# Two decoder layers on one core: the mixers rebuilt with transposed projections, heads on halves and quarters of the matmul array, gates spread by DMA, a new order and a new beginning

## Chip, core and metric

The kernel runs on one core of a Trainium2 chip. The metric is the device time of one execution in microseconds; lower is better. The core has a matmul engine (TensorE, PE in the profile, its weight loads PEld), a vector engine (VectorE, DVE), an engine for functions and copies (ScalarE, ACT), a general one (GpSimd, POOL) and one that issues DMAs (SyncE, SP). Matmuls read SBUF and write PSUM, which has eight banks of 128 x 512 fp32 here.

## The reference

x has 256 positions of width 1024. Each of two layers has three parts; ahead of each stands an RMS norm, behind each another, whose output is added to x.

```python
for l in range(DEPTH):                                   # 2
    h = rms_norm(x, pre_mix_g[l])
    x = x + rms_norm(parallel_mixer(h, ...), post_mix_g[l])
    h = rms_norm(x, pre_cross_g[l])
    x = x + rms_norm(memory_cross_attention(h, mem_n, ...), post_cross_g[l])
    h = rms_norm(x, pre_ffn_g[l])
    x = x + rms_norm(swiglu(h, w_gate[l], w_up[l], w_down[l]), post_ffn_g[l])

# parallel_mixer
lx, ly, fq, fk, fv, ff, rq, rk, rv, rg = split(h @ w_in)   # widths 256, 256, 512, 512, 512, 8, 256, 256, 256, 256
lru_out = rg_lru(causal_conv(lx), ...) * gelu(ly)          # gates of 4 blocks of 64, then a scan over positions
fox_out = forgetting_attention(fq, fk, fv, ff, ...)        # 8 heads of 64
ret_out = retention(rq, rk, rv, rg, positions)             # 4 heads of 64, rotary, decay, norm per head
return concat(lru_out, fox_out, ret_out) @ w_out

# forgetting_attention
c = cumsum(log_sigmoid(ff + b_f))                          # per head, over positions
logits = q k / 8 + c[query] - c[key], causal;  softmax;  times v
```

The cross-attention has 4 heads of 256 into 256 memory tokens; the feed-forward part has 2816 hidden columns.

## The kernel before

The 256 positions are two tiles t of 128. Every large product is made of three fp32r products: an operand is split into a high part (a cast, ACT) and a low part (the difference, DVE), and `mm3` multiplies high by high, high by low and low by high. Weights come from memory as pieces of 512 KB into `raw` (five buffers, issued by SP in `load`); `pump` splits a piece into `hi` and `lo` (eight buffers). `project` (positions on the partitions) has x stationary and 512 weight columns moving, once for each t; `project_t` (the output transposed, positions along the free side) has 128 weight columns stationary and the 256 positions of both tiles moving. The norm's factor rs, one number a position, is not multiplied into x but into what comes out of a projection: as a scalar on each partition after `project`.

The order of the work is set at build time by `Flow`: a model of each engine's clock with costs written in the kernel. The main line issues PE's big products; side tasks (generators that `yield` what they wait for) are woken when the model's PE clock has reached the time at which their inputs are ready, and `pump` and the tasks are asked after every few matmuls. What comes out is one fixed sequence for each engine, and each engine works through its own in order. PSUM banks and work tiles are taken from pools (`bank`, `work`).

In the mixer (`mixer`), the order of projections is fv_hi (half of v, and the 8 gate columns), fk, lru, fv_lo, fq, rqk, rvg, each for t = 0 and 1; then two blocks of memory keys (ck), then the output projection in the row order 0 to 7 (0, 1 LRU; 2 to 5 forgetting attention; 6, 7 retention). The names in the profile are: `acc` a projection's bank; `aug` q or k with two more columns that carry the gate's sum c, 66 in all, which `augmented` scales and `transposes` flips (bank `tr`, copied by ACT to `augT`); `lg` the logits' bank, which a bf16 product of an identity and `maskb` begins with the causal mask; `mx`, `pexp` the maximum and the exponentials; `pT` their flip; `fo` the values' bank, later divided by the sums and flipped; `lxy` the LRU's input scaled and then flipped; `rot` the rotated q and k of the retention, flipped to `rT`; `rsc` its scores (operands on partitions 0 to 63 or 64 to 127: half the array's rows); `ry` its output; `dn` an output projection; `mth`, `mtl` its left operand's high and low part. In the cross part the first block of memory values (cv) comes first, while the norm behind the output projection runs. In the program, matmuls are recorded at line 309, transposes at 321, DMAs at 229 and all else at 234.

At the beginning SP loads the first constants, x of tile 0, two weight pieces, x of tile 1, and further pieces; tile 0's x is flipped and split, and `second_tile` does the same for tile 1.

## Time and profile before

| | us |
|---|---|
| three runs, median (lowest, highest) | 850.97 (850.67, 852.89) |
| the profiled execution | 851.05 |
| its span, first to last instruction | 849.3 |
| PE busy, DVE busy, ACT busy, POOL busy | 837.3, 556.4, 436.2, 77.2 |
| mixer of layer 0 with memory keys, until dn begins | 16.3 to 125.3 |
| mixer of layer 1 with memory keys | 429.7 to 538.3 |

The mean granted clock is 0.996. A line of the profile's groups reads: line, engine, operation, tile written <- tiles read, shape, count | busy us, mean ns of one | idle time of the engine ahead of them and who ended it. A matmul's tiles are bank <- moving, stationary, and 64\*128 is the part of the array, rows by columns. Ends of matmuls are modelled, so the cost of one is read from start to start. A line of the timeline has the start, the length from the first start to the last end, engine, line and so on. Plain fp32 matmuls are recorded twice each.

### The profile page before, as it was taken

What the parts mean: (1) busy time and instruction counts of PE and PEld (TensorE: products, weight loads), DVE (VectorE), ACT (ScalarE), POOL (GpSimd) and SP (SyncE); (2) the same over time, 40 slices, a digit from 0 to 9 for tenths busy, and PEclk for the clock granted to TensorE, in tenths of its full rate; (3) what the DMA queues carried; (4) which work ended last, traced back from release to release, by engine and by line L of the source; (5) the groups of instructions that cost most, each with busy time, mean ns of one, the idle gap of its engine ahead of it and who ended that gap; (6) DMA issues with size and microseconds to landing.
All of it is one profiled execution on the core that took longest, in us unless ns stands there. A gap on an engine that the chain in (4) does not pass through costs nothing.

```text
span 849.3 us, 13416 instructions
## 1 busy us (share of the span) xinstructions
PE 837.3 (99%) x5329; PEld 749.8 (88%) x5329; DVE 556.4 (66%) x812; ACT 436.2 (51%) x666; POOL 77.2 (9%) x121
## 2 busy tenths in 40 slices
PE   7999999999999999999999999999999999999997
PEld 5888998999888999999888889889988899999995
DVE  5877886865577655557585776687566874656552
ACT  5479565555455434435365764465455653544431
POOL 2831211100020000000010201010001100000000
PEclk9999999999999999999999999999999999999999
DMA  8863525753457747557425523746443676647411
GB/s 277 306 215 102 174 79 172 225 196 100 149 167 242 239 138 232 183 141 226 147 100 174 174 79 121 223 148 226 147 151 103 223 237 205 198 144 232 146 51 50
DMA packets 92623, 145.25 MB, mean 171 GB/s; under 512 B 4768, under 2 KB 62240, under 8 KB 92432
## 3 DMA queue, kind: packets, MB, share of 16 engines
q1 hardware_dynamic: 91120, 138.65, 51.5%
q0 software_dynamic: 1440, 5.74, 1.9%
q8 instruction: 42, 0.69, 0.3%
q14 instruction: 21, 0.17, 0.1%
HBM read 143.32 MB, written 1.05 MB: 170 GB/s over the span
## 4 chain that ended last, share of the span: by engine, by line
PE 95%; DMA 1%; issue 1%; DVE 1%; ACT 1%; SPq 0%; DVEq 0%; POOLq 0%; POOL 0%; ACTq 0%
PE acc L309 60%; PE dn L309 24%; PE tr L321 4%; PE lg L309 2%; PE clg L309 1%; PE co L309 1%; PE fo L309 1%; DMA raw<-in_w_in 1%; PE ry L309 1%; DMA raw<-in_w_down 1%; SPq L229 0%; PE rsc L309 0%; PE gate L309 0%; ACT hi L234 0%; DVE lo L234 0%
## 5 line engine op out<-in xcount | busy, mean ns | idle before, releaser
L234 DVE TENSOR_TENSOR lo<-raw,hi 128x1024 fp32r<-128x1024 f32 (+1 forms) x244 | 292.1, 1220 | 151.3 <-ACT hi L234 150.6
L234 ACT CAST hi<-raw 128x1024 fp32r<-128x1024 f32 (+2 forms) x246 | 251.5, 1043 | 137.4 <-PE acc L309 93.8
L309 PE MATMUL acc<-xth,hi 128*128 128x256 f32 x704 | 198.9, 282 | 0.0
L309 PE MATMUL acc<-xth,lo 128*128 128x256 f32 x704 | 198.6, 282 | 0.0
L309 PE MATMUL acc<-xtl,hi 128*128 128x256 f32 x704 | 197.7, 281 | 0.0
L309 PEld LDWEIGHTS acc<-xth,hi 128*128 128x128 f32 x704 | 133.1, 189 | 0.9
L309 PEld LDWEIGHTS acc<-xtl,hi 128*128 128x128 f32 x704 | 133.0, 189 | 0.8
L309 PEld LDWEIGHTS acc<-xth,lo 128*128 128x128 f32 x704 | 133.1, 189 | 0.0
L309 PE MATMUL acc<-hi,xth 128*128 128x512 f32 (+2 forms) x288 | 111.4, 387 | 2.3 <-ACT xth L234 2.3
L309 PE MATMUL acc<-lo,xth 128*128 128x512 f32 (+2 forms) x288 | 106.8, 371 | 1.4 <-DVE lo L234 1.0
L309 PE MATMUL acc<-hi,xtl 128*128 128x512 f32 (+2 forms) x288 | 107.3, 372 | 0.4 <-DVE xtl L234 0.4
L309 PEld LDWEIGHTS acc<-hi,xth 128*128 128x128 f32 x288 | 54.9, 191 | 11.4 <-ACT xth L234 2.9
L309 PEld LDWEIGHTS acc<-hi,xtl 128*128 128x128 f32 x288 | 54.7, 190 | 10.5 <-DVE xtl L234 0.9
L309 PEld LDWEIGHTS acc<-lo,xth 128*128 128x128 f32 x288 | 55.0, 191 | 9.8 <-DVE lo L234 1.2
L234 POOL TENSOR_TENSOR rp<-ssp,mh 128x1 f32<-128x1 f32 x12 | 6.7, 559 | 545.8 <-DVE ssp L234 545.8
L309 PE MATMUL dn<-hi,mth 128*128 128x512 f32 x128 | 51.1, 399 | 0.0
L309 PE MATMUL dn<-hi,mtl 128*128 128x512 f32 x128 | 50.5, 394 | 0.0
L309 PE MATMUL dn<-lo,mth 128*128 128x512 f32 x128 | 50.3, 393 | 0.0
L309 PE MATMUL dn<-hi,gh 128*128 128x512 f32 x112 | 44.1, 394 | 0.0
L309 PE MATMUL dn<-hi,gl 128*128 128x512 f32 x112 | 44.1, 394 | 0.0
L309 PE MATMUL dn<-lo,gh 128*128 128x512 f32 x112 | 44.0, 393 | 0.0
L234 DVE TENSOR_TENSOR y<-dn,gpost 128x512 f32<-128x512 f32 x24 | 16.4, 687 | 34.2 <-ACT junk L234 34.2
(228 smaller groups left out, 1366.5 us busy)
## 6 DMA issues: line engine op xcount, KB each, us to landing
raw<-in_w_in SPq DMA_DIRECT2D x44, 512.0 KB, 4.6
raw<-in_w_gate SPq DMA_DIRECT2D x44, 512.0 KB, 4.6
raw<-in_w_up SPq DMA_DIRECT2D x44, 512.0 KB, 4.7
raw<-in_w_down SPq DMA_DIRECT2D x44, 512.0 KB, 4.6
raw<-in_w_ck SPq DMA_DIRECT2D x16, 512.0 KB, 4.6
raw<-in_w_out SPq DMA_DIRECT2D x16, 512.0 KB, 4.5
raw<-in_w_cv SPq DMA_DIRECT2D x16, 512.0 KB, 5.1
raw<-in_w_cq SPq DMA_DIRECT2D x16, 512.0 KB, 4.8
```

The costliest lines, as they stand in the source:

```text
L234: fn(*args, **kw)
L309: nc.tensor.matmul(out_ap, lhsT, rhs, start=start, stop=stop)
L321: nc.tensor.transpose(out_ap, src, ident[0:k, 0:k])
```

## The change

What is computed stays. In the mixers:

- lru, fk, fq and rqk become `project_t`, as two blocks of 256 columns each; fv and rvg stay `project`. `spread`, which was the feed-forward part's, makes rs along the free side (ones times a diagonal), and fk, lru are multiplied by it; q isn't scaled.
- Nothing of `aug` is left. q and k of a head lie on 64 partitions, two heads (e = 0, 1) on the two halves of the array's rows; the two heads' logits go to two banks. The gate's c[key] comes by another way: `gates` makes the sums transposed (8 x 256), DVE copies them, POOL writes them to memory by DMA, and reads them back in four DMAs that spread each row over 128 partitions (`far`). DVE then makes scaled logits plus far in `pexp`, takes the maximum of that, and after the exponentials multiplies by 1/sum ahead of the flip (c[query] cancels in the softmax).
- The values' product has v stationary, 64 columns on half the array's columns for each of two heads, and gives the transposed output, which needs no flip.
- The retention's w_in columns are reordered on the host, the cosine tables are made in transposed form (`turn`), and the scores go over 32 rows each, four heads on four quarters into four banks. rs is applied squared further down.
- The order is fv_hi, rvg, rqk, lru, fk, fq, fv_lo, and all three attention units (t = 0; t = 1 in two parts) come after the last. The first block of memory values is moved ahead of the output projection, whose rows are taken in the order 6, 7, 0, 1, ..., 5; the second half of the memory keys takes its place in the cross part.
- At the beginning the gains come as columns instead of rows to flip, tile 1's x comes in two DMAs, further constants by SP instead of POOL, and the first projection of layer 0 is `staged`: within a piece all high products first. The softplus of lambda goes with that of the gates.
- 24 work buffers instead of 21; less scratch for POOL's DMAs.

```diff
-        for name, c0, n in (("fv_hi", 1792, 264), ("fk", 1024, 512), ("lru", 0, 512), ("fv_lo", 1536, 256),
-                            ("fq", 512, 512), ("rqk", 2056, 512), ("rvg", 2568, 512)):
-            b[name] = columns(a["w_in"][l], c0, n, 2 if not blks and not b else None)
+        own = {"fv_hi": (1792, 264), "fv_lo": (1536, 256), "rvg": (2568, 512)}
+        flat = {"lru": 0, "fk": 1024, "fq": 512, "rqk": 2056}
+        b["in"] = ["fv_hi", "rvg", "rqk", "lru", "fk", "fq", "fv_lo"]
+        for name in b["in"]:
+            if name in own:
+                b[name] = columns(a["w_in"][l], *own[name], 2 if l == 0 and name == "fv_hi" else None)
+            else:
+                b[name] = [columns(a["w_in"][l], flat[name] + SEQ * h, SEQ) for h in (0, 1)]
...
-        b["mix_ks"] = [0, 1, 2, 3, 4, 5, 6, 7]
+        b["cv", 0] = columns(a["w_cv"][l], 0, 512)
+        b["mix_ks"] = [6, 7, 0, 1, 2, 3, 4, 5]
...
+        for k0 in range(0, KC if staged else 0, b.per):
+            ks = range(k0, k0 + b.per)
+            w = {k: weights(b, k, NT) for k in ks}
+            for i, j in ((0, 0), (0, 1), (1, 0)):
+                for k in ks:
+                    matmul(q[:, 0:b.n], x[i][:, k, :], w[k][j], k + i + j == 0, k == KC - 1 and i == 1)
+                flow.tick()
...
+        def gates():
+            yield list(lf)
+            b = bank("cum")
+            matmul(b[0:8, 0:P], lf[0], tri, True, True)
+            matmul(b[0:8, P:SEQ], lf[0], ones, True, False)
+            matmul(b[0:8, P:SEQ], lf[1], tri, False, True)
+            cT = work([8, SEQ], n="cT")
+            V.tensor_copy(cT, b[0:8, 0:SEQ])
+            yield cT
+            dr = dp.tile([8, SEQ], F32, tag="cum", name=nm("cum"), bufs=2)
+            PO.dma_start(out=dr, in_=cT)
+            yield dr
+            for e in range(2):
+                for g in range(2):
+                    far[e, g] = work([P, 2, SEQ], n="far")
+                    PO.dma_start(out=far[e, g], in_=dr[4 * e + 2 * g:4 * e + 2 * g + 2, :].partition_broadcast(P))
...
-                        matmul(b[:, j * P:(j + 1) * P], qT[t][g][0:66, h, :], kT[kt][g][0:66, h, :], False, j == n - 1)
+            for e in range(2):
+                matmul(bs[e], identb, maskb[:, 512 * t:512 * t + 512], True, False)
+            for i, j in enumerate(js):
+                for e in range(2):
+                    r = slice(64 * e, 64 * e + 64)
+                    matmul(bs[e][:, i * w:(i + 1) * w], qT[j // 2][r, j % 2, t * P:(t + 1) * P],
+                           kT[j // 2][r, j % 2, 0:w], False, i == n - 1)
...
+                    V.scalar_tensor_tensor(pv[:, i:i + 2], bv[:, i:i + 2], xt[t].by[HD ** -0.5], far[e, g][:, :, 0:w],
+                                           op0=ALU.mult, op1=ALU.add)
+                V.tensor_reduce(mx[t][:, o:o + n], pv, axis=AX, op=ALU.max, negate=True)
...
-                        matmul(fo[:, o:o + HD], et[:, i * (t + 1) + kt, :], v[kt][:, o:o + HD], kt == 0, kt == t)
+            for i, j in enumerate(js):
+                for kt in range(t + 1):
+                    for e in range(2):
+                        o = (2 * j + e) * HD
+                        matmul(fo[t][64 * e:64 * e + 64, j * P:(j + 1) * P], v[kt][:, o:o + HD],
+                               pT[e][:, i * (t + 1) + kt, :], kt == 0, kt == t)
...
+                for c in range(2):
+                    for h in range(4):
+                        r = slice(32 * h, 32 * h + 32)
+                        matmul(bs[h][:, o:o + n], rot[1][r, c, kt * P:kt * P + P], rot[0][r, c, kt * P:SEQ],
+                               c == 0, c == 1)
...
-    for c in range(2):
-        SY.dma_start(out=X[0][:, 512 * c:512 * c + 512], in_=a["x"][0, 0:P, 512 * c:512 * c + 512])
-    load(2)
-    SY.dma_start(out=X[1], in_=a["x"][0, P:2 * P, :])
+    for t in range(NT):
+        for c in range(2):
+            cut = slice(512 * c, 512 * c + 512)
+            SY.dma_start(out=X[t][:, cut], in_=a["x"][0, t * P:t * P + P, cut])
+        load(2 + 2 * t)
+    SY.dma_start(out=cst[:, C_FIRST:C_SOON], in_=a["pack"][:, C_FIRST:C_SOON])
```

How the order moves is shown at three places. First PE in layer 0, at the logits of the first 128 positions. Before, they stand within the second fq block; `augT` are the flipped q and k.

```order
L309 LDWEIGHTS maskb_75
L309 MATMUL lg_928<-maskb_75 128x512
L309 MATMUL lg_928<-augT_612,augT_841 128x128 x4
L309 LDWEIGHTS maskb_75
L309 MATMUL lg_940<-maskb_75 128x512
L309 MATMUL lg_940<-augT_619,augT_848 128x128 x4
```

Now they stand behind the last projection (the first row is the end of fv_lo), both masks first.

```order
L316 MATMUL acc_1197<-hi_980,xtl_103 128x256
L316 LDWEIGHTS maskb_77
L316 MATMUL lg_1234<-maskb_77 128x512
L316 LDWEIGHTS maskb_77
L316 MATMUL lg_1235<-maskb_77 128x512
L316 MATMUL lg_1234<-kT_862,qT_1027 128x128
L316 MATMUL lg_1235<-kT_862,qT_1027 128x128
```

The last two rows go on in turn, eight in all: one head in each bank, on the two halves of the rows, and no flip of q or k ahead of them.

Second DVE at the beginning. Before, the second tile's `xg` (flipped x times the gain, 187 and 200) stand behind the low part of the fifth weight piece (`lo_178`).

```order
L234 TENSOR_TENSOR lo_130<-raw_86,hi_129 128x528
L234 TENSOR_TENSOR xtl_100<-xg_137,xth_99 128x512
L234 TENSOR_TENSOR lo_156<-raw_91,hi_155 128x528
L234 TENSOR_TENSOR lo_178<-raw_95,hi_177 128x1024
L234 TENSOR_TENSOR xg_187<-tr_182,cols_77 128x512
L234 TENSOR_TENSOR xg_200<-tr_195,cols_77 128x512
L234 TENSOR_TENSOR xtl_100<-xg_187,xth_99 128x512
```

Now they are 182 and 196, and stand ahead of the fourth and the fifth piece (`lo_202`, `lo_223`).

```order
L240 TENSOR_TENSOR lo_173<-raw_93,hi_172 128x528
L240 TENSOR_TENSOR xg_182<-tr_177,cst_76 128x512
L240 TENSOR_TENSOR xg_196<-tr_191,cst_76 128x512
L240 TENSOR_TENSOR xtl_103<-xg_182,xth_102 128x512
L240 TENSOR_TENSOR xtl_103<-xg_196,xth_102 128x512
L240 TENSOR_TENSOR lo_202<-raw_95,hi_201 128x528
L240 TENSOR_TENSOR lo_223<-raw_98,hi_222 128x1024
```

The second tile has moved ahead by two splits; POOL, which did two low parts before, does none now.

Third POOL in layer 1, between the norm behind layer 0 (`rstd`, `f`) and the LRU (`lg_4902`, `lg_5198`: here the gelu's argument). Before:

```order
L234 TENSOR_SCALAR ss_4615<-ss_4615 128x1
L234 TENSOR_TENSOR rstd_4525<-ss_4615,mh_76 128x1
L234 TENSOR_SCALAR f_4620<-rstd_4525 128x1
L234 TENSOR_SCALAR lg_4902<-lg_4902 128x512
L234 TENSOR_TENSOR lg_4902<-lg_4902,lyT_4805 128x512
```

Now, from the last of five such factors on:

```order
L240 TENSOR_SCALAR f_4707<-rstd_4609 128x1
L235 DMA cum_4963<-cT_4914 8x256
L235 DMA far_5007<-cum_4963 128x512
L235 DMA far_5009<-cum_4963 128x512
L235 DMA far_5011<-cum_4963 128x512
L235 DMA far_5013<-cum_4963 128x512
L240 TENSOR_TENSOR rn_5158<-var_5157,mh_78 128x4
L240 TENSOR_TENSOR rn_5170<-var_5169,mh_78 128x4
L240 TENSOR_SCALAR lg_5198<-lg_5198 128x512
```

The DMAs of the gates have come between, and the retention's norm (`rn`), which stood at the mixer's end, now stands ahead of the LRU's steps.

## The prediction

> **What bounds the kernel now.** I read the page first, for the shares, then the busy time by stage, then the chain of waits, and then the timeline at places where PE changes its kind of work.

> ```profile
> span 849.3 us, 13416 instructions
> PE 837.3 (99%) x5329; PEld 749.8 (88%) x5329; DVE 556.4 (66%) x812; ACT 436.2 (51%) x666; POOL 77.2 (9%) x121
> ...
> 0.00:16.00 16.00, 11.15 (x54) 6.95 (x54) 7.61 (x13) 6.73 (x11) 3.34 (x7) 1.00 0.89 283
> 16.00:19.40 3.40, 3.18 (x15) 3.15 (x15) 2.39 (x4) 3.40 (x6) 1.07 (x3) 0.50 0.76 268
> ...
> 30.00:125.00 95.00, 95.00 (x616) 84.25 (x615) 75.39 (x157) 63.39 (x120) 25.70 (x40) 1.00 0.48 158
> ...
> 441.00:538.30 97.30, 97.30 (x625) 86.11 (x625) 69.69 (x136) 57.40 (x109) 11.52 (x13) 1.00 0.42 136
> ```

> The two stretches 30 to 125 and 441 to 538 us are the two mixers (with the memory keys); the columns are length, then busy PE, PEld, DVE, ACT, POOL, clock, DMA. PE is busy for all of both, at the full clock, and DVE, the next, for 79% and 72%. But a PE that is "busy" by modelled ends proves little; what counts is whether one matmul starts as soon as the one before allows. The chain of waits gives that: runs of equal matmuls, start and length.

> ```profile
> 332.69 5.58 PE dn L309 x24
> ...
> 389.28 22.84 PE acc L309 x192
> ```

> A matmul with 512 moving columns costs 5.58/24 = 0.2325 us, one with 256 columns 22.84/192 = 0.119 us. With these prices, and those for the small fp32 matmuls below, I added up PE's program by stage: from 20 us on the sum of prices and the clock agree to about 2 us in 820. So PE never waits to speak of, and each microsecond of PE work that the change adds or takes away inside a mixer moves the end, as long as nobody makes PE wait instead. That is the whole argument; the rest is prices. The profiled execution took 851.05 us, 1.75 more than its span; the median of the three runs, 850.97, is 0.1 beside it. I reckon from 851.05. About 0.3% (2.5 us) is what can be told from no change.

> **The change part by part: PE's work.** Both layers together.

> ```profile
> L309 PE MATMUL acc<-hi,xth 128*128 128x512 f32 x224 | 91.7, 409 | 0.0
> ...
> L309 PE MATMUL lg<-augT,augT 66*128 66x128 f32 x96 | 12.7, 275 | 0.0
> ...
> L309 PE MATMUL fo<-fv,pT 128*128 128x64 f32 x96 | 12.0, 269 | 0.0
> ...
> L321 PE MATMUL tr<-cst,aug 128*66 128x128 f32 x64 | 8.3, 272 | 0.0
> ```

> Projections: four blocks of 512 columns a layer turn from project to project_t. That is 128 of these 224 in each of the three products gone, 384 x 0.2325 = -89.3, and 768 of 256 columns instead, 768 x 0.119 = +91.4: together +2.1.

> Transposes: 64 for aug go, and 16 each for lxy, rot and fo (four a flip, two positions, two layers), 112 in all.

> ```profile
> 104.54 0.28 PE L309 MATMUL acc<-memh,lo 128*128 128x256 f32 x1
> 104.66 0.60 PE L321 MATMUL tr<-cst,fo 128*128 128x128 f32 x4
> 105.01 0.36 PE L309 MATMUL acc<-memh,hi 128*128 128x256 f32 x1
> 105.22 0.28 PE L309 MATMUL acc<-meml,hi 128*128 128x256 f32 x1
> ```

> From the start of the transposes to the second matmul behind them are 0.56 us, of which one matmul is 0.12: 0.44 for four, 0.11 each. So -12.3, with +0.4 for the four of the cosine tables and -0.2 for the two of the gains: -12.1.

> Attention, retention and gates: these are plain fp32, two records a matmul.

> ```profile
> 73.80 1.06 PE L309 MATMUL lg<-augT,augT 66*128 66x128 f32 x8
> 74.69 0.38 PE L309 MATMUL lg<-maskb 128*128 128x512 bf16 x1
> ...
> 497.21 1.89 PE L309 MATMUL fo<-fv,pT 128*128 128x64 f32 x16
> 498.94 0.38 PE L309 MATMUL lg<-maskb 128*128 128x512 bf16 x1
> ...
> 61.53 1.03 PE L309 MATMUL gate<-xc,cst 128*128 128x256 f32 x4
> 62.39 0.27 PE L321 MATMUL tr<-cst,msrc 128*128 128x128 f32 x1
> ...
> 100.51 1.05 PE L309 MATMUL lg<-augT,augT 66*128 66x128 f32 x8
> 101.50 0.71 PE L309 MATMUL rsc<-rT 64*128 64x128 f32 x8
> 102.05 0.61 PE L309 MATMUL rsc<-rT,rT 64*128 64x128 f32 x8
> 102.59 1.10 PE L309 MATMUL ry<-rv,rsc 128*128 128x64 f32 x8
> ```

> By differences of starts, a logits record costs 0.89/8 = 0.111 us, a value record 1.73/16 = 0.108 (few columns are no cheaper), and one with 256 columns 0.86/4 = 0.215. The retention scores show what half the array does: 16 records on alternating halves of the rows take 1.09 us, where 16 on the full array would take 1.78. So two halves run side by side, a pair in 0.112 (8 pairs, 0.90), and the change of shape costs the rest: 0.19 here, and 0.10 in the logits ahead (0.99 where 0.89 is usual), 0.29 a run.

> Logits: 96 x 0.111 = 10.7 before. Afterwards a head is 64 rows on one half: for the first 128 positions 16 pairs of records at 0.112, for the rest 16 pairs of 256 columns at 0.215: 5.2, so -5.5. The masks' 12 matmuls stay. Values: 96 x 0.108 = 10.4 before; then 48 pairs of 128 columns on halves of the columns, 48 x 0.112 = 5.4: -5.0. Halves of the columns stand in no row; the nearest are those halves of the rows, and the other bound is no overlap, 10.8. Retention scores: 24 pairs (2.7) become 8 groups of four at 0.215 and 8 at 0.112 (2.6): -0.1, and +2.5 if quarters run only two at a time. The product of ones and diag, once more a layer, is two matmuls, four records: +0.9. Changes of shape: four runs before; afterwards three of logits, three of values, one of scores and one of gates a layer, 16, so 12 more x 0.29 = +3.5, between nothing, since a run on columns may change for less, and 7.0, twice the row.

> The sum is +2.1 - 12.1 - 5.5 - 5.0 - 0.1 + 0.9 + 3.5 = **-16.2 us**.

> [...]

> **The beginning.**

> ```profile
> 10.50 0.71 DVE L234 TENSOR_TENSOR lo<-raw,hi 128x528 fp32r<-128x528 f32 x1 [1.28 <-ACT hi L234]
> ...
> 11.92 1.05 ACT L234 CAST hi<-raw 128x1024 fp32r<-128x1024 f32 x1 [0.72 <-DMA raw<-in_w_in]
> 13.00 1.22 DVE L234 TENSOR_TENSOR lo<-raw,hi 128x1024 fp32r<-128x1024 f32 x1 [1.79 <-ACT hi L234]
> 14.14 1.28 DVE L234 TENSOR_TENSOR xg<-tr,cols 128x512 f32<-128x512 f32 x2
> 14.86 1.22 ACT L234 CAST xth<-xg 128x512 fp32r<-128x512 f32 x2 [1.89 <-DVE xg L234]
> 15.51 1.29 DVE L234 TENSOR_TENSOR xtl<-xg,xth 128x512 fp32r<-128x512 f32 x2
> 15.53 0.39 PE L309 MATMUL acc<-hi,xth 128*128 128x264 f32 x1 [2.00 <-ACT xth L234]
> ...
> 20.44 0.39 PE L309 MATMUL acc<-hi,xth 128*128 128x512 f32 x1
> ```

> Here DVE stands in the fifth weight piece's low part, which waits for ACT and that for the DMA, and the second tile's x waits behind it; PE idles 2.0 us, falls to half clock (the 0.50 above) and begins the next block at 20.44. In the new order both halves of the second tile stand ahead of that piece. DVE would come to them after the third piece, at about 11.2, be through at 12.6, ACT's copies at 13.2 and the low parts at 14.0; the fourth piece's split, now behind them, some 0.7 on either engine like the first row, ends at 14.7, the first tile's product at 15.0, and 24 matmuls of 0.12 later the next block begins at 17.9: -2.5. Bounds: nothing (the half clock falls on it again) and -4.2 (the second tile begins at 13.3). [...]

> **What I cost at nothing.** The gates' way through memory: a small DMA out, a wait of POOL for it, four of 256 KB back, and POOL's rotary steps stand behind that wait. The nearest row is the gain's broadcast of twice the size:

> ```profile
> gpost<-in_post_mix_g POOLq DMA_DIRECT2D x2, 512.0 KB, 4.6
> ```

> Even five in series are 23 us; between the gates' product and the first logits lie some 40 us of projections (seven halves at 5.7). If that cover were gone it would cost up to 23 us a layer. The split of w_in in pieces of 4x256 has the same bytes and the same two casts. cv moved ahead of the output projection is replaced by ck as cover for the norm behind it, 48 x 0.2325 = 11.2 against 96 x 0.119 = 11.4 us. ACT loses its copies of augT, lxy and rT; DVE trades scaling for biasing and normalizing.

> **New waits.** All three attention units now come after the last projection, beside the end of the LRU, the memory's splits and the second norm.

> ```profile
> L234 DVE TENSOR_TENSOR lo<-raw,hi 128x1024 fp32r<-128x1024 f32 x240 | 288.1, 1223 | 148.8 <-ACT hi L234 148.1
> ...
> L234 ACT ACTIVATION_READ_ACCUMULATOR pexp<-lg,mx 128x1 f32 x32 | 6.6, 207 | 0.0
> ...
> L234 ACT ACTIVATE pexp<-lg,mx 128x128 f32<-128x128 f32 x16 | 5.6, 378 | 0.8 <-DVE mx L234 0.8
> ...
> L234 DVE TENSOR_REDUCE mx<-lg 128x2 f32<-128x512 f32 x8 | 5.4, 687 | 1.9 <-PE lg L309 1.9
> ...
> L234 DVE TENSOR_TENSOR rsc<-rsc,cst 128x256 f32<-128x256 f32 x4 | 1.6, 419 | 1.0 <-PE fo L309 1.0
> ```

> In layer 0, from the first logits to the low part of the first unit's output, DVE has 10 splits (12.2), six reductions (4.1), eight passes of 512 at 0.69 (5.5), four of 256 at 0.42 (1.7) and 19 smaller ones of 0.15 to 0.69 (9.9): 33.4 us, against some 27 of PE. It falls 6 behind, and PE has 13 more until it needs that output. I take +1.5 us for waits here, between 0 and 8. With it: 851.05 - 16.2 - 2.5 + 1.5 = **834 us**.

> **Rivals.** (1) Columns or quarters do not overlap: values +5.4, scores +2.5, so 842. For it: no row shows either; against: halves of the rows do to the nanosecond. (2) DVE is late in layer 0 and PE waits out all of the 6.1: 839, with the same in layer 1, 845. (3) **Slower**: the attention chain itself becomes the end of each mixer. One unit by rows is logits 2, biasing 1.7, maximum 1.4, eight exponentials of 0.38 and 0.21 for their sums (4.7), normalizing 1.5, flips and copies 2.1, values 1, split 1.3: 15.6 us, the others 12 each, 40 in series. PE needs the last one 39 us after the projections (22.6 of keys and values, 16.8 of output products). If 16 weight splits of 1.22 also stand between the steps, it is 20 us late a layer: 873. It decides from 8.5 us a layer. Against it: the order has each unit's logits ahead of the former's flips, and 2 to 3 us of other work between steps. (4) The change doesn't do what it says: a change of shape costs 1.4 us, not 0.29, on columns, and eats all 17: 851.

> **Chances.** Forecast 0.62, (1) 0.15, (2) 0.16, (3) 0.04, (4) 0.03. Low end: changes of shape free (-3.5) and the beginning at -4.2, 834 - 3.5 - 1.7 - 1.5 = 827. High end: rival (1), 842, which also holds the first case of (2). Faster is all but (3) and (4): 0.93.

> **What would show it.** Right: PE still without gaps in both mixers; logits pairs at 0.112 and 0.215, values pairs at 0.112, scores by fours, about 0.29 around each run; 112 transposes fewer; the block after fv_hi beginning near 18 us; each mixer some 7 to 8 us shorter. Wrong: values records at 0.11 one after the other; PE idle before tr of pexp, before dn, or before lo of a weight piece late in the mixer; PE waiting for the flip of the cosine tables, which POOL's wait for the gates delays.

## The result, and the profile after

| | before | after |
|---|---|---|
| median of four runs (lowest, highest), us | 851.62 (850.67, 852.89) | 838.60 (837.69, 839.43) |
| ratio after to before, 95% interval | | 0.9846 (0.9826, 0.9866) |
| span of the profiled execution, us | 849.3 | 836.1 |

The kernel is faster by 1.5%, 13.0 us between the medians. The forecast was 834, 17 us faster, in a range of 827 to 842: the time lies inside, and a good 4 us of the expected gain are missing. They are what there is to find.

The page of the profile after, and its busy time by stage (length, then busy PE, PEld, DVE, ACT and POOL, clock, DMA): the stretch behind the beginning's gap, the mixer of layer 0, and the mixer of layer 1.

```profile
span 836.1 us, 13940 instructions
PE 822.3 (98%) x5589; PEld 745.2 (89%) x5591; DVE 565.9 (68%) x779; ACT 426.4 (51%) x639; POOL 93.7 (11%) x144
```

```profile
14.90:18.30 3.40, 3.40 (x18) 3.40 (x17) 2.36 (x2) 3.40 (x5) 3.23 (x5) 0.51 0.78 218
...
30.00:125.00 95.00, 92.59 (x739) 85.95 (x740) 80.04 (x123) 58.91 (x102) 33.60 (x42) 1.00 0.58 188
432.00:532.00 100.00, 99.49 (x788) 91.61 (x786) 82.88 (x137) 57.12 (x102) 17.55 (x22) 1.00 0.52 163
```

Before, PE was busy for 95.00 of 95 us in the first mixer; now 2.4 us are idle there, while the second is as full as it was: its 0.5 us of idle time lies at its very start, at 433 to 434 us, where the kernel before has the same at 439 to 440. And the half clock, which stood at 16.0 to 19.4 us, now stands at 14.9 to 18.3.

To see what each stage gave, I take the same place in both timelines: the product that spreads the norm's factor in the feed-forward part of each layer. Before, and then after, with the second block's first matmul:

```profile
267.69 0.67 PE L309 MATMUL rsb<-diag,cst 128*128 128x256 f32 x2
682.25 0.60 PE L309 MATMUL rsb<-diag,cst 128*128 128x256 f32 x2
```

```profile
19.58 0.40 PE L316 MATMUL acc<-hi,xth 128*128 128x512 f32 x1
261.88 0.60 PE L316 MATMUL rsb<-diag,cst 128*128 128x256 f32 x2
668.47 0.60 PE L316 MATMUL rsb<-diag,cst 128*128 128x256 f32 x2
```

The beginning, until the block after fv_hi, gave 20.44 - 19.58 = 0.9 us. From there to the first of these products it was 247.25 and is 242.30: 4.9 less, of which 0.4 was a wait of PE at that very place before. From the first to the second it was 414.56 and is 406.59: 8.0 less. From the second to the end it is 0.6 more (167.0 to 167.6), and so it is in every trace of a changed kernel (167.5 to 167.7): 0.4 of it lies behind the issue of the last output DMAs, at 845.64 before and 832.08 after; the cause is open. Together 13.2, the difference of the spans. Each mixer should have given 8: layer 1 did, layer 0 gave some 3.4 too little, and the beginning 1.6 too little.

Layer 1's timeline of PE, around the scores, the first logits, the second logits and the first values (start, length, count of records):

```profile
462.41 1.59 PE L316 MATMUL rsc<-rot,rot 32*128 32x256 f32 x32
463.93 0.39 PE L316 MATMUL acc<-xth,hi 128*128 128x256 f32 x1
...
502.61 1.16 PE L316 MATMUL lg<-kT,qT 64*128 64x128 f32 x16
503.70 0.38 PE L316 MATMUL acc<-memh,hi 128*128 128x256 f32 x1
...
510.39 1.13 PE L316 MATMUL lg<-kT,qT 64*128 64x256 f32 x8
511.46 0.39 PE L316 MATMUL acc<-memh,hi 128*128 128x256 f32 x1
...
523.77 1.09 PE L316 MATMUL fo<-pT,fv 128*64 128x128 f32 x16
524.79 0.51 PE L316 MATMUL acc<-hi,memh 128*128 128x512 f32 x1
```

From the start of a run to the next matmul: 16 records of logits in 1.09 us, 8 of double width in 1.07, 16 of values in 1.02, 32 of scores (half of them of double width) in 1.52. By pairs of 0.112 and 0.215 the first three are 0.90, 0.86 and 0.90, by fours the scores are 1.31. So halves of the rows, halves of the columns and quarters of the rows all run side by side in full, and what is over, 0.12 to 0.21, with some 0.1 in the matmul ahead or behind, is the change of shape.

Layer 0 has the waits. PE first, with what ended the idle time in brackets, then DVE, then POOL at the same time:

```profile
53.91 0.66 PE L332 MATMUL tr<-cst,msrc 128*128 128x128 f32 x4 [0.34 <-ACT msrc L240]
...
70.58 0.39 PE L316 MATMUL acc<-xth,hi 128*128 128x256 f32 x1 [0.34 <-DVE kT L240]
...
96.63 0.41 PE L332 MATMUL tr<-cst,yc 128*128 128x128 f32 x2 [0.48 <-DVE yc L240]
...
98.27 0.39 PE L316 MATMUL acc<-meml,hi 128*128 128x256 f32 x1 [1.12 <-DVE meml L240]
```

```profile
90.45 1.63 DVE L240 TENSOR_TENSOR lo<-raw,hi 128x1024 fp32r<-128x1024 f32 x1
92.01 0.83 DVE L240 TENSOR_TENSOR yc<-yc,rn 128x256 f32<-128x256 f32 x1
92.76 2.29 DVE L240 TENSOR_TENSOR lo<-raw,hi 128x1024 fp32r<-128x1024 f32 x1
94.97 1.51 DVE L240 TENSOR_TENSOR yc<-yc,rn 128x256 f32<-128x256 f32 x1
96.41 1.21 DVE L240 TENSOR_TENSOR lo<-raw,hi 128x1024 fp32r<-128x1024 f32 x1
97.54 0.68 DVE L240 TENSOR_TENSOR meml<-xg,memh 128x512 fp32r<-128x512 f32 x1
```

```profile
90.19 0.82 POOL L240 TENSOR_SCALAR ld<-t 128x512 f32<-128x512 f32 x1
90.99 1.57 POOL L240 TENSOR_SCALAR rec<-rec 128x512 f32<-128x512 f32 x1
92.65 1.32 POOL L240 TENSOR_TENSOR ld<-ld,rec 128x512 f32<-128x512 f32 x1
...
94.57 1.62 POOL L240 TENSOR_TENSOR li<-li,lr 128x512 f32<-128x512 f32 x1
```

A split that takes 1.21 us when POOL is quiet takes 1.63 and 2.29 beside POOL's passes over the LRU's tiles, and a product of 0.42 takes 0.83 and 1.51: four instructions of DVE, 3.0 us too long. PE then waits for yc and for the memory's low part, which stand behind them. Counted from start to start, beyond a matmul's price, the four waits are 0.5, 0.5, 0.65 and 1.36: 3.0 us; with two of 0.23 ahead of the masks it is the 3.4 that are missing.

### The profile page after: what moved, and what is told of

It is laid out like the page before. It is cut to its first block, busy times and chain, and to the rows that moved or that the text cites. A ratio compares the mean times of both kernels' runs of the same rounds, so it can differ in the third digit from the quotient of the medians.

```text
span 836.1 us, 13940 instructions
## 1 busy us (share of the span) xinstructions
PE 822.3 (98%) x5589; PEld 745.2 (89%) x5591; DVE 565.9 (68%) x779; ACT 426.4 (51%) x639; POOL 93.7 (11%) x144
## 3 DMA queue, kind: packets, MB, share of 16 engines
HBM read 145.59 MB, written 1.06 MB: 175 GB/s over the span
## 4 chain that ended last, share of the span: by engine, by line
PE 87%; DVE 4%; POOL 3%; DMA 2%; issue 2%; ACT 2%; SPq 0%; DVEq 0%; POOLq 0%; ACTq 0%
PE acc L316 55%; PE dn L316 24%; PE tr L332 2%; DVE lo L240 1%; PE clg L316 1%; PE co L316 1%; DMA raw<-in_w_in 1%; POOL ang L240 1%; PE lg L316 1%; PE fo L316 1%; DMA cum<-cT 1%; ACT hi L240 1%; POOL f L240 0%; DVE yc L240 0%; DVE soft L240 0%
## 5 line engine op out<-in xcount | busy, mean ns | idle before, releaser
L240 DVE TENSOR_TENSOR lo<-raw,hi 128x1024 fp32r<-128x1024 f32 (+2 forms) x246 | 299.1, 1234 | 143.8 <-ACT hi L240 143.0
L316 PE MATMUL acc<-xth,hi 128*128 128x256 f32 x960 | 272.9, 284 | 0.3 <-DVE kT L240 0.3
L316 PE MATMUL acc<-xth,lo 128*128 128x256 f32 x960 | 271.0, 282 | 0.0
L316 PE MATMUL acc<-xtl,hi 128*128 128x256 f32 x960 | 269.5, 281 | 0.0
L316 PEld LDWEIGHTS acc<-xth,hi 128*128 128x128 f32 x960 | 181.5, 189 | 2.1 <-DVE kT L240 0.5
L316 PEld LDWEIGHTS acc<-xtl,hi 128*128 128x128 f32 x960 | 181.5, 189 | 1.0
L316 PEld LDWEIGHTS acc<-xth,lo 128*128 128x128 f32 x960 | 181.5, 189 | 0.0
L316 PE MATMUL acc<-hi,xth 128*128 128x512 f32 (+2 forms) x160 | 57.0, 360 | 2.0 <-ACT hi L240 1.6
L316 PE MATMUL acc<-lo,xth 128*128 128x512 f32 (+2 forms) x160 | 56.2, 355 | 0.8 <-DVE lo L240 0.8
L316 PE MATMUL acc<-hi,xtl 128*128 128x512 f32 (+2 forms) x160 | 56.1, 355 | 0.2 <-DVE xtl L240 0.2
## 6 DMA issues: line engine op xcount, KB each, us to landing
raw<-in_w_in SPq DMA_DIRECT2D x44, 512.0 KB, 5.1
raw<-in_w_gate SPq DMA_DIRECT2D x44, 512.0 KB, 4.3
raw<-in_w_up SPq DMA_DIRECT2D x44, 512.0 KB, 4.6
raw<-in_w_down SPq DMA_DIRECT2D x44, 512.0 KB, 4.6
raw<-in_w_ck SPq DMA_DIRECT2D x16, 512.0 KB, 4.0
raw<-in_w_cv SPq DMA_DIRECT2D x16, 512.0 KB, 4.6
raw<-in_w_out SPq DMA_DIRECT2D x16, 512.0 KB, 3.8
raw<-in_w_cq SPq DMA_DIRECT2D x16, 512.0 KB, 4.7
```

The costliest lines, as they stand in the source:

```text
L240: fn(*args, **kw)
L316: nc.tensor.matmul(out_ap, lhsT, rhs, start=start, stop=stop)
```

## The experiments

Theory: the arithmetic of PE's work holds; what is missing was lost to PE's clock in the beginning and to waits in layer 0, most of them made by POOL's passes, which hold DVE up. Rivals: DVE has too much work of its own where the attention was put; the side-by-side parts are cheaper by themselves; changes of shape cost more than 0.29 us. Eleven rows, the first of them the changed kernel itself, each against runs of the kernel before on its chip:

| kernel | median, us | ratio to before, 95% interval |
|---|---|---|
| changed, again | 837.73 | 0.9851 (0.9832, 0.9869) |
| changed, gap filled | 838.39 | 0.9851 (0.9835, 0.9867) |
| changed, POOL's products left out | 836.16 | 0.9825 (0.9809, 0.9840) |
| changed, POOL's products on DVE | 836.55 | 0.9833 (0.9818, 0.9848) |
| changed, heads one by one | 841.60 | 0.9889 (0.9873, 0.9906) |
| changed, masks in pieces | 839.92 | 0.9870 (0.9855, 0.9885) |
| changed, gates' DMAs later | 837.27 | 0.9838 (0.9823, 0.9853) |
| three edits (gap, DVE, DMAs) | 835.62 | 0.9821 (0.9806, 0.9836) |
| two edits (gap, DMAs) | 837.14 | 0.9831 (0.9817, 0.9844) |
| three edits, memory's norm earlier | 833.97 | 0.9794 (0.9781, 0.9808) |
| before, gap filled | 849.55 | 0.9978 (0.9969, 0.9987) |

Intervals are some 0.3% wide, and edits of 1 us are 0.12%: where they overlap, the trace decides and not the ratio.

**The changed kernel again.** No edit.

> The changed kernel once more, as the base of the three that run beside it. Both theories: 838.6 us as before, within 1 us.

Its profiled execution took 836.19 us, and it shows something else at the beginning than the first one did:

```profile
14.90:18.30 3.40, 3.40 (x28) 3.27 (x27) 2.53 (x3) 3.40 (x6) 3.16 (x6) 1.00 0.80 205
```

The same 3.40 us hold 28 matmuls at full clock where they held 18 at 0.51, and the block after fv_hi begins at 17.55 us. Same program, the same 1.6 us of idle time of PE ahead of it (from 11.6 to 13.2): so the half clock is not a property of the kernel but of the execution. Not all of the 2.0 us between the two blocks is its doing: this execution is 0.5 us ahead already before the gap. The four waits of layer 0 are all there, the one for msrc at 0.85 instead of 0.5.

**The gap filled.**

```diff
         for k0 in range(0, KC if staged else 0, b.per):
...
+            for _ in range(8 if k0 == 6 else 0):
+                nc.tensor.matmul(wb, warm[:, 0:P], warm, start=True, stop=True)
             for i, j in ((0, 0), (0, 1), (1, 0)):
```

> The changed kernel with eight products on zeros (512 columns in bf16, 0.216 us each) on PE ahead of the fourth weight piece's first matmul, where PE idles from 11.9 to 13.7 us; all else stands in the same order. Theory (the beginning gains only 0.9 us since that idle time brings the half clock, which then falls on the second tile's 24 matmuls): no stretch of 0.5, those matmuls at 0.12 instead of 0.22, the block after fv_hi from 18.1 instead of 19.6 us, total -1.4 us. Rival (the second tile's start and not the clock is what holds): the block begins at 19.6 as now, 0. If the fillers themselves are late: up to +0.5.

The products on zeros fill the gap, and further down a stretch at half clock is found in another place:

```profile
14.00:17.90 3.90, 3.60 (x30) 3.53 (x30) 2.39 (x3) 3.90 (x7) 2.78 (x4) 1.00 0.82 253
...
98.10:101.50 3.40, 3.40 (x19) 3.40 (x18) 3.30 (x8) 3.00 (x12) 0.00 (x0) 0.52 0.57 228
```

The beginning went as the theory had it: no half clock, the block at 17.87 us. But the total did not move: 838.39, where 837.2 was expected. 3.4 us at half clock now follow layer 0's waits at 95 to 97.6 us and cost 1.6 (17 matmuls, 0.094 each), and the wait for msrc at 51.8 us has grown from 0.5 to 1.3 us, since PE comes earlier and POOL does not. How often that stretch comes is open: only one execution was traced.

**POOL's products left out, and on DVE.** The four products of two tiles in each LRU:

```diff
-            PO.tensor_tensor(d, d, r, op=ALU.mult)
+            skip(0.3 + 2.3e-3 * 512, d, r)
```

```diff
-            PO.tensor_tensor(d, d, r, op=ALU.mult)
+            VP.tensor_tensor(d, d, r, op=ALU.mult)
```

`skip` only books the planner's cost; `VP` is DVE, booked as POOL, so that the order of everything else stays.

> The changed kernel without POOL's four two-operand passes in each LRU (the gelu's product, the decay's and the two of the gated input are left out; the LRU's output is then another). All other engines have the same instructions in the same order. Theory A (these passes hold up DVE: beside them a split of 1.22 takes 1.63 and 2.29 us, a product of 0.42 takes 0.83 and 1.51, and PE in layer 0 then waits 0.65 for yc, 1.36 for meml and 0.5 for kT): DVE's passes there have their usual length, the three waits go, -2 to -2.5 us. Rival B (DVE has too much work of its own between the last projection and the logits of the second unit): the waits stay, 0 to -0.5.

> The changed kernel with the same four passes of each LRU given to DVE, at the same places of its program; nothing is left out. Theory A (they cost DVE more as holds than as work): DVE gets 4 x 0.69 = 2.8 us of work a layer and loses some 4.7 us of holds in layer 0, so PE waits 1 to 2 us less, -1 to -2. Rival B (DVE's own work is the limit there): +1 to +2.8 us in layer 0, and up to as much in layer 1.

DVE without the products, at the place shown above:

```profile
89.14 1.63 DVE L240 TENSOR_TENSOR lo<-raw,hi 128x1024 fp32r<-128x1024 f32 x1
90.69 0.83 DVE L240 TENSOR_TENSOR yc<-yc,rn 128x256 f32<-128x256 f32 x1
91.44 1.21 DVE L240 TENSOR_TENSOR lo<-raw,hi 128x1024 fp32r<-128x1024 f32 x1
92.58 0.41 DVE L240 TENSOR_TENSOR yc<-yc,rn 128x256 f32<-128x256 f32 x1
```

The second split and the second product are back at 1.21 and 0.41; the first of each still stand beside the two passes that stayed on POOL (ld, rec), and still cost 0.41 each too much. PE no longer waits for yc or meml, and half as long for kT. The LRU's products were the cause of these waits: theory A holds. From the block after fv_hi to the end it is 814.2 us against 816.5, so -2.4 with 2 to 2.5 expected. The three waits make 2.3 of it; besides, the wait for msrc (0.5) is gone, since the gates' DMAs, 17 us ahead of the first product left out, happened to be issued 2.4 us earlier in this execution, and a wait of 0.2 in the feed-forward part is new. With the products on DVE the waits for kT and yc are gone too, but the one for meml stays (DVE's rows, then PE's):

```profile
89.61 0.69 DVE L240 TENSOR_TENSOR ld<-ld,rec 128x512 f32<-128x512 f32 x1 [1.49 <-POOL rec L240]
...
94.90 0.69 DVE L240 TENSOR_TENSOR meml<-xg,memh 128x512 fp32r<-128x512 f32 x1
```

```profile
95.64 0.38 PE L317 MATMUL acc<-meml,hi 128*128 128x256 f32 x1 [0.93 <-DVE meml L240]
```

That looks like a share for theory B, but the first row says otherwise. The product `ld` now stands on DVE ahead of the splits and waits for `rec`, a pass that stayed on POOL: DVE is idle for 1.49 us there and then works without a break to meml, for which PE waits 1.2 us beyond a matmul's price. The idle time is longer than the wait, so DVE's own work would have let meml be in time: the wait that stays comes from POOL again, by way of the order; the kernel with the three edits has the same idle time (1.50). Expected were -1 to -2; against the changed kernel beside it the medians give -1.2, while the traced execution, counted from the block after fv_hi, gives nothing (816.5), for it has a new wait of 0.65 in the feed-forward part and a longer one for msrc (0.8 instead of 0.5).

**Heads one by one.** Logits, values and scores are issued with all matmuls of one part of the array first:

```diff
+            raw = []
             for i, j in enumerate(js):
                 for e in range(2):
                     r = slice(64 * e, 64 * e + 64)
-                    matmul(bs[e][:, i * w:(i + 1) * w], qT[j // 2][r, j % 2, t * P:(t + 1) * P],
+                    later(raw, e, bs[e][:, i * w:(i + 1) * w], qT[j // 2][r, j % 2, t * P:(t + 1) * P],
                            kT[j // 2][r, j % 2, 0:w], False, i == n - 1)
+            one_by_one(raw)
```

`later` books the matmul with the planner, `one_by_one` issues the list sorted by e; values and scores likewise.

> The changed kernel with the heads of one run of logits, of values and of scores no longer in turn: all matmuls of one half or quarter of the array first, then those of the next. Same matmuls, same banks, same count of shape changes. Theory (parts of the array run side by side only when neighbours in the program lie on different parts): logits 5.2 to 10.5, values 5.4 to 10.8, scores 2.6 to 10.5, so +18.5 us. Rival (a matmul on a part of the array is cheaper by itself, or PE looks ahead): 0.

PE's timeline of this kernel in layer 1, at the scores, the two runs of logits shown before, and the first values:

```profile
464.14 1.71 PE L339 MATMUL rsc<-rot,rot 32*128 32x256 f32 x32
...
504.45 1.71 PE L339 MATMUL lg<-kT,qT 64*128 64x128 f32 x16
506.09 0.39 PE L316 MATMUL acc<-memh,hi 128*128 128x256 f32 x1
...
512.81 1.14 PE L339 MATMUL lg<-kT,qT 64*128 64x256 f32 x8
513.88 0.39 PE L316 MATMUL acc<-memh,hi 128*128 128x256 f32 x1
...
526.20 1.58 PE L339 MATMUL fo<-pT,fv 128*64 128x128 f32 x16
```

A miss: 18.5 us were expected, and the kernel is 3 to 4 us slower (ratio 0.9889 against 0.9851). My theory that only neighbours in the program overlap is wrong. Where a part has four records in a run, nothing or little is lost: the wide logits take 1.07 us as before, the second half's first record starting 13 ns after the first half's, and the scores, two such runs, 1.64 instead of 1.52 (the next matmul starts at 465.78). Where it has eight, half of the overlap is lost: 16 logits take 1.64 us instead of 1.09. In the records of that run the first half goes alone for four, the second joins at the fifth, and the last four of the second go alone: 12 x 0.112 + change. That reads as if PE went on past up to four waiting records of one part to begin the next part's; the depth is only argued from these two lengths, and which half a record belongs to is read from the program's order, since the records don't say it. That it is the overlap which makes the gain, and not a cheaper small matmul, the same records show: alone, each costs the full 0.11.

**Masks in pieces.**

```diff
-            for e in range(2):
-                matmul(bs[e], identb, maskb[:, 512 * t:512 * t + 512], True, False)
             for i, j in enumerate(js):
+                for e in range(2):
+                    o = 512 * t + i * w
+                    matmul(bs[e][:, i * w:(i + 1) * w], identb, maskb[:, o:o + w], True, False)
                 for e in range(2):
```

> The changed kernel with the causal mask laid in pieces ahead of each pair of heads instead of one product a bank ahead of all: the three runs of logits a layer become eight, ten more changes of shape in all. Theory (0.29 us a change): +2.9 us, and up to +0.5 for the mask in smaller pieces. Rival (1.4 us a change): +14. Rival (a change is free): 0 to +0.5.

In layer 1, from the first mask of t = 0 to the matmul behind the last pair:

```profile
502.86 0.29 PE L845 MATMUL lg<-maskb 128*128 128x128 bf16 x2
503.07 0.49 PE L316 MATMUL lg<-kT,qT 64*128 64x128 f32 x4
...
505.42 0.39 PE L316 MATMUL acc<-memh,hi 128*128 128x256 f32 x1
```

2.56 us, and 1.63 in the changed kernel (its masks start at 502.07, the next matmul at 503.70): 0.93 for three more runs, 0.31 each. The price of 0.29 holds, and neither 1.4 nor nothing. The kernel is 1.3 to 2.2 us slower by the medians, not 2.9: in layer 0 PE's longer way is in part taken out of its waits, which are 1.4 us shorter in all in this trace (the one for yc and the two ahead of the masks are gone, meml's is 1.1).

**The gates' DMAs later.** In layer 0 POOL issues the four `far` DMAs behind the memory's first factor:

```diff
-                    PO.dma_start(out=far[e, g], in_=src)
+                    behind.append((far[e, g], src))
```

In `memory_norm` the list is issued behind `scale_norm`; layer 1 is as it was.

> The changed kernel with POOL issuing the four DMAs that spread the gates in layer 0 behind the first memory norm's factor instead of ahead of it; all else stands in the same order. Theory (PE's 0.5 us ahead of the memory's flip at 53.3 us come from POOL's wait for the gates' way through memory, which holds that factor back by 3 us): the wait goes, -0.5 us, and the gates, 45 us early, cost nothing. Rival (the wait is ACT's own load there): 0. If the gates weren't early: slower.

POOL's factor in the changed kernel, and then PE and POOL with the DMAs later:

```profile
47.87 2.24 POOL L235 DMA_DIRECT2D far<-cum  x4 [0.97 <-DMA cum<-cT]
...
52.10 0.57 POOL L240 TENSOR_TENSOR rstd<-ss,mh 128x1 f32<-128x1 f32 x1
```

```profile
48.71 0.57 POOL L240 TENSOR_TENSOR rstd<-ss,mh 128x1 f32<-128x1 f32 x1
```

```profile
53.49 0.60 PE L332 MATMUL tr<-cst,msrc 128*128 128x128 f32 x4
```

The factor comes at 48.71 instead of 52.10 and PE no longer waits for the flip (no bracket). The theory holds; the medians (-0.5 against the changed kernel's second one) agree but could not decide it.

**Edits together.** First the gap filled, the products on DVE and the DMAs later; then the same without DVE; then the first with the second memory tile's norm begun earlier (`MEM_AT = (45, 50)` instead of `(45, 55)`).

> The three edits together: PE filled in the gap of the beginning, POOL's four passes of each LRU on DVE, the gates' DMAs behind the first memory norm. If all three theories hold: -1.4 -1.5 -0.5 = -3.4 against the changed kernel, 835.2 us. If only the clock's: -1.4, 837.2. If DVE's own work is the limit: 838 to 841.

> The changed kernel with the gap of the beginning filled and the gates' DMAs behind the first memory norm; the LRU's passes stay on POOL. Theory (with PE 1.7 us earlier, the waits for kT, yc and the memory's low part stay at 2.4 us, since POOL's passes hold DVE; and these 2 us of idle time bring the half clock there in some executions): 836.5, 0.9 above the kernel with the passes on DVE. Rival (POOL's holds cost nothing that DVE's work would not): 835.6, the same as with the passes on DVE.

> The kernel with the three edits together, and the second memory tile's norm begun 5 us earlier by the planner's clock, which puts the last low part of the memory ahead of four splits instead of behind them in DVE's program. Theory (the wait of 1.2 us for that low part at 94 us is DVE's order, now that POOL holds nobody): the wait goes, no idle time of PE over 0.5 us is left in layer 0's mixer, -1.2 us against the three edits, 834.4. Rival (DVE is full there and another low part is late instead): 0.

Three edits: 835.62, with 835.2 expected. Without DVE's share 837.14, and PE's waits for kT, yc and meml are back in its trace; the half clock behind them was not in it. By the medians the products on DVE are worth 1.5 us, by the ratios 0.9; the intervals overlap. With the memory's norm earlier it is 833.97, 834.4 expected, ratio 0.9794 (0.9781, 0.9808), clear of the changed kernel's in both its measurements: the fastest here, 4 us less than the change alone and 17.6 less than before. But this edit does more than its expectation says. The planner now puts the last `meml` at 81.94 us instead of 94.79, and the LRU's product `ld` at 75.46 instead of 89.50, where DVE no longer waits for POOL; so the gain over the three edits is that of a new order in this stretch, and what the memory's norm alone gives is not shown. The mixer of layer 0 is then as full as it was before the change:

```profile
30.00:125.00 95.00, 95.00 (x750) 88.03 (x749) 83.47 (x135) 60.16 (x105) 25.39 (x38) 1.00 0.61 198
```

**The kernel before, gap filled.** Ten products on zeros ahead of the second tile's first matmul.

> The kernel before, with ten products on zeros on PE ahead of the second tile's first matmul, where PE idles from 13.4 to 15.5 us; all else as it was. Theory (the half clock after idle time of 2 us is nothing of the change; it comes in most executions and costs 12 to 17 matmuls 0.1 us each): no stretch of 0.5, the block after fv_hi from 19.0 instead of 20.44, -1.4 us in the profile and about -1 in the median, 850. Rival (it comes at a fixed time whatever PE does): 0.

PE's timeline there:

```profile
13.21 2.33 PE L977 MATMUL warm<-warm 128*128 128x512 bf16 x10
...
18.94 0.39 PE L309 MATMUL acc<-hi,xth 128*128 128x512 f32 x1
```

The block begins at 18.94 as expected, and the median is 2.1 us lower, 0.2% (0.1 to 0.3), where about 1 was expected. At 16.0 to 19.4 us, where the clock was 0.50, it is 1.00 in this execution. So the half clock was in the kernel before as well, and it did not come at that moment when PE's gap ahead of it was filled.

## Why the prediction was right, and where it was not

**PE's work, -16.2: right.** Layer 1 has no waits and shows the prices pure. There I summed the time from each matmul's start to the next one's, by kind, from the end of its first block (438.6 us before, 432.7 after) to the feed-forward part (663.2 and 649.4). Projections, the memory's too: 137.7 before, 138.0 after, +0.3 where +1.05 a layer was put. Flips: 12.3 to 7.2, -5.1 for 56 fewer, where -6.2 was put; flips and projections have to be read together, since part of a flip's 0.11 was the slower matmul behind it. Logits with masks -1.6, values -2.1, scores -0.2, changes of shape in all three: -3.9 where -3.6 was put. Gates and the spread factor +0.5, as put; all other kinds together +0.3. Sum -7.9 a layer, with -8.2 forecast for this one: the error of this term is about half a microsecond over both layers. Four quarters and two halves overlap in full here, by the 1.52 and 1.02 us above, in runs of 128 and 256 columns.

**The beginning, -2.5: the order right, the clock left to chance.** The step was "24 matmuls of 0.12 later the next block begins at 17.9". Where the clock stayed up it began at 17.55; in the first profile 15 of those matmuls took 0.22 and it began at 19.58. The gap of PE did not go, it moved: from the second tile's x to the fourth piece's high part, which ACT now makes behind two copies of x. The prediction named this as its bound ("the half clock falls on it again"), but took the middle value as if it were one number, and that value set a block before at half clock against one after at the full. Like with like it is 20.44 to 19.58 with the half clock and 18.94 to 17.55 and 17.87 without it (the gap filled before; open and filled after): 0.9 to 1.4 from the new order, in single executions whose matmuls ahead of the gap start up to 1.4 us apart. The rest of the 2.5 is the half clock's 1.5 (20.44 to 18.94 in the kernel before), which comes or stays away with the execution.

Of eight traced executions with an open gap of 1.6 to 2 us, six had a stretch at half clock behind it (3.4 us long, from 13.5 to 16.0 us on; in one it began within the gap and met only nine matmuls) and two had none; of the five with a filled gap none had. The traces also show what goes with the one and the other. In the first profiles of before and after the half clock lasts 3.413 us, and the clock falls again 826.03 and 815.79 us after its end, 242 and 239 times that length; it begins at 16.00 and 14.96 us, so this grid of 3.41 us lies at another place in each. In the six the gap lay within the 3.41 us ahead of the half clock, but for 0.15 us at most, and PE was busy for 39 to 47% of them. In the two a border of the grid cut the gap, and PE was busy for 63% and more on both sides. Such a stretch in the first profile after, and the emptier one of the changed kernel's second (the second number is PE's busy time):

```profile
11.55:14.96 3.41, 1.47 (x9) 1.05 (x9) 2.84 (x5) 3.04 (x6) 0.15 (x1) 1.00 1.04 380
```

```profile
9.22:12.64 3.42, 2.15 (x14) 1.54 (x12) 2.78 (x5) 1.85 (x4) 0.00 (x0) 1.00 1.07 384
```

**New waits, +1.5: too small, and by another way.** The step that failed is "it falls 6 behind, and PE has 13 more until it needs that output". I added up DVE's instructions at their usual lengths and looked for the wait at the attention's output. The attention never made PE wait, unless the two of 0.23 ahead of its masks are its doing. DVE was late because POOL's passes held it, 3 us in that stretch, and what came late was the retention's yc and the memory's last low part. I could have known: in the trace of before, DVE's `meml` takes 1.10 us instead of 0.69 and `rot` 1.32 instead of 0.42 at 82 to 86 us, beside the same passes of POOL, only that nobody waited for it there. Two of DVE's instructions ended only behind POOL's products beside them: the split at 92.76 ends 1.08 us after POOL's product beside it (93.97), the product at 94.97 ends 0.28 after the next one (96.20), and the split on DVE without POOL beside it is back at 1.21 us.

**Costed at nothing.** The gates' way through memory was indeed hidden: the tiles lie ready 40 us early. But what is queued behind POOL's wait was named incompletely. I wrote of the rotary steps; behind two of them stands the memory's factor, and that cost PE 0.5 us, more when PE comes earlier (1.3 with the gap filled).

**The sum.** Forecast -17.2 against -13.2 of the spans: 1.6 are missing in the beginning, most of it by the clock, 1.9 went to waits beyond the 1.5, 0.5 to prices; the 0.6 at the end and the wait of 0.4 that was there before nearly cancel. The time lies in the range, but nearer to rival (2), 839, than to 834, and that rival came about in part: DVE was late in layer 0 and PE waited for it. Its number is met by chance, though. PE waited 2.5 to 3.0 us for DVE and not 6.1, not at the attention's output, and mostly because of POOL's passes; the clock and the prices made up the rest. The other rivals did not come about: columns and quarters overlap (16 records of values in 1.02 us, 32 of scores in 1.52), the attention chain was never late, a change costs 0.31.

## What to carry to other kernels

When PE is full, add up its instructions: that part of a forecast held to half a microsecond in sixteen. Price every instruction of the helpers beside what will run at the same time, since a DVE pass beside a POOL pass took up to 3.6 times its usual length here (1.51 us for 0.42); and look in the old trace for instructions that are sometimes too long without harm, since a new order can put them on the path. PE's idle gap of 2.0 us in the kernel before cost 1.5 us more than itself by the half clock (20.44 against 18.94 us), while two of eight executions with a gap of 1.6 to 2 us had none; with products on zeros in it the clock stayed at 1.00 there in all five kernels that have them, but that shows in the time only when the next wait does not take it back.
